# A hybrid S5 and Conformer layer: the convolution's tap diagonals get a room of their own and are made one channel block ahead

## The chip, the cores and the metric

The kernel runs on one core of one Trainium2 chip. The metric is the device time of one execution in microseconds (us), lower is better. Before the change it is 888.91 us, the median of three runs that lay between 885.72 and 889.24 us.

Engines are named as the profile names them: PE is TensorE (matmuls, with PEld for its weight loads), DVE is VectorE, ACT is ScalarE, POOL is GpSimd, and SP issues most of the transfers.

## The reference

One layer of a diffusion backbone, on 512 latent tokens and 256 context tokens of width 1024, all in float32:

```python
h = modulate(rmsnorm(x, g_mix), sh1, sc1)          # sh, sc, gt: six vectors from cond @ w_ada
z = h @ w_in                                       # 3584 columns
y_a = s5_post(s5_mixer(z[:, :512], ...))           # state-space branch, two directions, 32 groups
y_b = conv_branch(z[:, 512:1536], 8 rows, ...)     # the convolution branch
x = x + gt1 * (g_a * y_a + g_b * y_b) @ w_o        # g_a, g_b: sigmoid of the other columns of z
h = modulate(rmsnorm(x, g_ffn), sh2, sc2)
x = x + gt2 * hier_moe(h)                          # 4 groups of 8 experts, top 2 within one group
out = rmsnorm(x, g_final)
```

The part that the change is in:

```python
def conv_branch(zb, n_rows, w_dw, b_dw, ln_g, ln_b, w_out):
    v = glu(zb)                                    # 512 tokens x 512 channels
    v = v.reshape(8, 64, 512)                      # 8 grid rows of 64 tokens
    v = depthwise_conv(v, w_dw, width 31, 'SAME') + b_dw
    v = silu(layernorm(v, ln_g, ln_b))
    return v.reshape(512, 512) @ w_out
```

The convolution is depthwise: each of the 512 channels has 31 weights (taps) of its own and mixes no other channel.

## The kernel before

**Stages.** First the condition vectors, the norms and the first part of the input projection (to about 104 us); then a mixed stage (to about 400 us) in which eight blocks of the state-space branch, 24 tiles of the rest of the input projection and the convolution are interleaved; then the output projections, the routing and 32 experts.

**The convolution on PE.** The 512 channels are four channel blocks of 128 channels on the partitions. The gated input of a block stands in `vp`, 8 rows of 64 tokens with 15 zeros at both ends of each row; `vp[0]` (pool tag `ch`) holds blocks 0 and 1, `vp[1]` (tag `cl`) blocks 2 and 3. `conv_diag(j)` (L786) builds the taps of block j as small diagonal matrices on DVE: two instructions (L792), one for taps 0 to 15 (128x512) and one for taps 16 to 30 (128x480), each an identity pattern `sel32` times the weights `cwt`. `conv_taps(j)` (L795) then issues 31 x 4 = 124 matmuls at L804 (as the profile counts them 248, since a float32 matmul is two), each with one 32x32 diagonal as weights and a shifted view of `vp` as the moving operand. The four matmuls of one tap are for the four quarters of 32 channels, r = 0 to 3, and each quarter has a PSUM bank of its own: `cp0` and `cp1` from the pool tag `mm` (4 banks), `cp2` and `cp3` from the tag `tp` (2 banks). ACT copies the four banks out (L808), and `conv_sum(j)` (L811) adds up the four partial sums in each bank with PE (`pcv`, L814).

**Where it stands.** `z_tile(t)` (L754) computes one 128-column tile of the projection in 24 matmuls (`zp`, L396 to L398; as tiles z0, z1, ... below). Behind tiles 2, 4, 6 and 8 follows `conv_taps` of blocks 0, 1, 2 and 3, behind tiles 3, 5, 7 and 9 their `conv_sum` (`conv_part`, L818). PE and ACT take their instructions in the order in which the code is written, through the letters of the string at L928 (`A`, `B`, `C` are z tiles, `R` and `I` the state-space block's read and input, `P` its tables, `V`, `b`, `k` its kernels, `a` a step of the condition vector's matmul or sum). DVE, POOL and SP are ordered by a scheduler.

**What shares DVE and the banks with it.** Per state-space block, DVE takes four products of PSUM tiles with cosines and sines (L669 to L672), two scans (L681), four more products (L686 to L689) and `st` (L95). It also splits the projection's weights (`zuwl`, L752), gates `vp` (L771), and finishes the block's convolution kernel `ks`: L553 is the last reader of the bank `pk` of the tag `tp`, and its result is what SP writes out with `kd` (L554) and reads back as `m` (L558).

**Pools.** The diagonals `cdg` came from the pool tag `s2`, a ring of eight 2 KB buffers per partition that also serves `sg`, `cpt`, the state-space products and others. So a buffer of the ring can make a later instruction wait for its last reader.

Of the kernel before, what the change touches and what calls it, by code (L numbers as in the profile page):

```python
# [9 lines left out]
F32 = mybir.dt.float32  # L10
# [4 lines left out]
ALU = mybir.AluOpType  # L15
# [11 lines left out]
def hybrid_kernel(  # L27
# [9 lines left out]
    V, S, G, T, SY = nc.vector, nc.scalar, nc.gpsimd, nc.tensor, nc.sync  # L37
# [10 lines left out]
    ROWS, RW = 8, 64  # L48
    PADW = RW + 2 * HALF
# [9 lines left out]
    modp = ctx.enter_context(tc.tile_pool(name="modp", bufs=1))  # L59
# [7 lines left out]
    def t2k(name, dt=F32, cols=512, p=128):  # L67
        return sm.tile([p, cols], dt, tag="s2", name=name)
# [4 lines left out]
    def ps_mm(name, p=128):  # L73
        return ps.tile([p, 512], F32, tag="mm", name=name, bufs=4)
# [4 lines left out]
    def ps_tp(name, p=128):  # L79
        return ps.tile([p, 512], F32, tag="tp", name=name, bufs=2)  # L80
# [114 lines left out]
    sel32 = sm.tile([128, 32], F32, tag="sel32", name="sel32", bufs=1)  # L195
# [4 lines left out]
    cwt = const.tile([128, 4, 32], F32, name="cwt")  # L200
# [452 lines left out]
    def s5_ut(b):  # L653
        if b < NB:
            uts[b] = s5m.tile([128, GB, NCH], F32, tag="ut", name="ut", bufs=2)
            SY.dma_start(out=uts[b], in_=ud[b // 2, 64 * (b % 2):64 * (b % 2) + 64].rearrange("(g q) t n -> (q t) g n", q=CH))
# [67 lines left out]
        V.tensor_tensor(yl[:, j, :], y, yh.bitcast(F32)[:, j, :], op=ALU.subtract)  # L724


    vp = [modp.tile([128, 2, ROWS, PADW], F32, tag=t, name=f"vp{t}") for t in ("ch", "cl")]
    for a in vp:
        G.memset(a, 0.0)


    zt = []
# [49 lines left out]

    cdg, cpart = {}, {}

    def conv_diag(j):
        cdg[j] = []
        for k0 in (0, 16):
            n = min(16, TAPS - k0)  # L790
            t = t2k("cdg").rearrange("p (k c) -> p k c", c=32)
            V.tensor_tensor(t[:, 0:n], sel32.unsqueeze(1).to_broadcast([128, n, 32]), cwt[:, j, k0:k0 + n].unsqueeze(2).to_broadcast([128, n, 32]), op=ALU.mult)  # L792
            cdg[j].append(t)

    def conv_taps(j):  # L795
        src = vp[j // 2][:, j % 2]
        conv_diag(j)
        d = cdg.pop(j)
        banks = [ps_mm("cp0"), ps_mm("cp1"), ps_tp("cp2"), ps_tp("cp3")]
        for k in range(TAPS):  # L800
            c = 32 * (k % 4)
            for r in range(4):
                rs_ = slice(32 * r, 32 * r + 32)
                T.matmul(banks[r][c:c + 32], lhsT=d[k // 16][rs_, k % 16, :], rhs=src[rs_, :, k:k + RW], start=(k < 4), stop=(k >= TAPS - 4), skip_group_check=True)  # L804
        cpart[j] = []
        for r in range(4):
            t = t2k("cpt")
            S.activation(t, banks[r], AF.Copy)  # L808
            cpart[j].append(t)
# [7 lines left out]
    def conv_part(t):  # L817

        if 2 <= t < 10:
            (conv_sum if t % 2 else conv_taps)((t - 2) // 2)  # L820
# [62 lines left out]
    def ada(n):  # L883

        for _ in range(n):
# [3 lines left out]
                ada_step(at[0])  # L889
            at[0] += 1  # L890

    s5_ut(0)
    s5_ut(1)
    for t in range(4):
# [396 lines left out]
    n = 0  # L1291
# [133 lines left out]
    with tc.If(n_gen > 0):  # L1425
        with tc.For_i(0, n_gen, 1):
# [16 lines left out]
            n = 0  # L1443
# [15 lines left out]
            def w_part(q):  # L1459
                t = mo.tile([128, 2048], F32, tag="er", name="gw", bufs=3)[:, 0:1024]  # L1460
                if q < 4:
                    v = t.rearrange("p (k a n) -> p k a n", k=2, a=2)
                    for a in range(2):
                        SY.dma_start(out=v[:, :, a, :], in_=ws[a][256 * q:256 * q + 256].rearrange("(k p) n -> p k n", p=128))
                else:
                    SY.dma_start(out=t, in_=ws[2][128 * (q - 4):128 * (q - 4) + 128])
                return t
# [11 lines left out]
            for q in range(4):  # L1479
                t = w_part(q)  # L1480
# [11 lines left out]
            for k in range(2):  # L1492
                t = w_part(4 + k)
# [220 lines left out]
```

## Time and profile before

| | |
|---|---|
| median of three runs | 888.91 us |
| profiled execution's own time | 891.78 us |
| its span (first to last instruction) | 890.1 us |
| PE busy | 746.9 us (84%) |
| DVE busy | 465.8 us (52%) |
| POOL busy | 331.7 us (37%) |
| ACT busy | 321.7 us (36%) |
| mean granted TensorE clock | 0.943 |

The profile is of one execution, and the share of a busy engine is a mean over stages that have different limits. What matters for this change is the stage from 105 to 250 us, where the four convolution blocks stand on PE at 142, 168, 202 and 231 us. A number in brackets at a row's end is the idle time of the engine just before it, with what ended it.

### The profile page before, as it was taken

What the parts mean: (1) busy time and instruction counts of PE and PEld (TensorE: products, weight loads), DVE (VectorE), ACT (ScalarE), POOL (GpSimd) and SP (SyncE); (2) the same over time, 40 slices, a digit from 0 to 9 for tenths busy, and PEclk for the clock granted to TensorE, in tenths of its full rate; (3) what the DMA queues carried; (4) which work ended last, traced back from release to release, by engine and by line L of the source; (5) the groups of instructions that cost most, each with busy time, mean ns of one, the idle gap of its engine ahead of it and who ended that gap; (6) DMA issues with size and microseconds to landing.
All of it is one profiled execution on the core that took longest, in us unless ns stands there. A gap on an engine that the chain in (4) does not pass through costs nothing. (4 is left out here: it accounts for less than half of the span.)

```text
span 890.1 us, 14314 instructions
## 1 busy us (share of the span) xinstructions
PE 746.9 (84%) x5486; PEld 519.6 (58%) x5486; DVE 465.8 (52%) x723; ACT 321.7 (36%) x559; POOL 331.7 (37%) x293
## 2 busy tenths in 40 slices
PE   3598976988889997779999993788998988888895
PEld 0476853665566775646778872455655655555542
DVE  4948464564387797826875576133223123233254
ACT  3443611353555766637732330222112112212133
POOL 4657435343576788631610122122123122122400
PEclk9998996998988999999999996799999999999997
DMA  8926860341145546478687447999989998997042
GB/s 310 263 61 177 206 214 20 107 125 30 57 135 172 169 129 182 130 248 303 210 299 274 151 132 313 397 380 364 377 321 388 407 350 342 387 389 261 27 178 94
DMA packets 84678, 202.01 MB, mean 227 GB/s; under 512 B 12859, under 2 KB 42621, under 8 KB 74866
## 3 DMA queue, kind: packets, MB, share of 16 engines
q1 hardware_dynamic: 76754, 180.00, 57.3%
q0 software_dynamic: 5856, 12.45, 4.0%
q10 hardware_dynamic: 1984, 8.44, 3.5%
q8 instruction: 53, 0.87, 0.4%
q14 instruction: 31, 0.25, 0.1%
HBM read 180.16 MB, written 26.69 MB: 232 GB/s over the span
## 5 line engine op out<-in xcount | busy, mean ns | idle before, releaser
L1346 PE MATMUL peg<-eraw,st 128*64 128x256 f32 x1152 | 133.7, 386 | 9.5 <-PEq L1407 7.4
L1346 PEld LDWEIGHTS peg<-eraw,st 128*64 128x64 f32 x1152 | 94.7, 139 | 60.4 <-issue 34.8
L1331 DVE COPY st<-pxt 128x512 f32<-128x512 f32 x32 | 22.1, 692 | 160.0 <-PE pxt L1329 160.0
L1360 ACT ACTIVATE at<-pat 128x256 f32<-128x256 f32 x32 | 12.3, 384 | 215.8 <-PE pat L1358 215.8
L1318 POOL DMA_INDIRECT xg<-h2d,tb x32 | 30.4, 950 | 141.3 <-PE pxt L1329 129.6
L396 PE MATMUL zp<-hh,zuwh 128*128 128x512 f32 x192 | 78.7, 410 | 0.0
L398 PE MATMUL zp<-hh,zuwl 128*128 128x512 f32 x192 | 77.1, 401 | 0.5 <-POOL zuwl L752 0.3
L397 PE MATMUL zp<-hl,zuwh 128*128 128x512 f32 x192 | 76.8, 400 | 0.0
L1366 PE MATMUL ped<-eraw,at 128*64 128x512 f32 x288 | 68.9, 603 | 0.0
L98 POOL TENSOR_TENSOR adacc<-adacc,wa 128x512 f32<-128x512 f32 x30 | 47.1, 1570 | 39.9 <-ACT wa L854 37.6
L1376 DVE TENSOR_TENSOR ye<-ped,gt2h 128x512 f32<-128x512 f32 x60 | 39.0, 687 | 40.2 <-PE ped L1366 37.3
L1401 POOL DMA_INDIRECT ybuf<-ye,ixh x34 | 34.0, 999 | 69.5 <-DVE ye L1376 49.8
L1329 PE MATMUL pxt<-ident,xg 128*128 128x128 f32 x256 | 42.4, 303 | 8.1 <-DMA xg<-h2d,tb 7.4
L396 PEld LDWEIGHTS zp<-hh,zuwh 128*128 128x128 f32 x192 | 37.4, 195 | 11.9 <-issue 4.4
L398 PEld LDWEIGHTS zp<-hh,zuwl 128*128 128x128 f32 x192 | 37.2, 194 | 9.8 <-POOL zuwl L752 1.8
L397 PEld LDWEIGHTS zp<-hl,zuwh 128*128 128x128 f32 x192 | 37.1, 193 | 7.4
L1329 PEld LDWEIGHTS pxt<-ident,xg 128*128 128x128 f32 x256 | 33.6, 194 | 13.1 <-issue 8.6
L1358 PE MATMUL pat<-ident,sge 64*128 64x64 f32 x128 | 21.3, 286 | 18.9 <-PEq L1407 18.2
L1358 PEld LDWEIGHTS pat<-ident,sge 64*128 64x128 f32 x128 | 17.7, 209 | 32.7 <-PEq L1407 30.4
L1366 PEld LDWEIGHTS ped<-eraw,at 128*64 128x64 f32 x288 | 17.8, 136 | 27.2 <-issue 23.6
L98 POOL TENSOR_TENSOR vb<-vta,vtb 128x512 f32<-128x512 f32 x16 | 22.3, 1393 | 30.0 <-PE pv L533 19.1
L752 DVE TENSOR_TENSOR zuwl<-zr,zuwh 128x1024 fp32r<-128x1024 f32 x16 | 28.4, 1775 | 5.7 <-ACT zuwh L751 5.6
(494 smaller groups left out, 1666.9 us busy)
## 6 DMA issues: line engine op xcount, KB each, us to landing
eraw<-in_w_exp_gate_dram SPq DMA_DIRECT2D x24, 1024.0 KB
eraw<-in_w_exp_up_dram SPq DMA_DIRECT2D x24, 1024.0 KB
eraw<-in_w_exp_down_dram SPq DMA_DIRECT2D x24, 1024.0 KB
wa<-in_w_ada_dram SPq DMA_DIRECT2D x32, 512.0 KB
zr<-in_w_in_dram SPq DMA_DIRECT2D x12, 1024.0 KB
wa<-in_w_ada_dram SPq DMA_DIRECT2D x8, 1024.0 KB
eraw<-in_w_exp_gate_dram SPq DMA_DIRECT2D x14, 512.0 KB
eraw<-in_w_exp_down_dram SPq DMA_DIRECT2D x14, 512.0 KB
```

Source lines behind the costliest of these rows:

```text
L98: G.tensor_tensor(o, a, b, op=op)
L396: T.matmul(acc, lhsT=wh, rhs=ah, start=start, stop=False)
L397: T.matmul(acc, lhsT=wh, rhs=al, start=False, stop=False)
L398: T.matmul(acc, lhsT=wl, rhs=ah, start=False, stop=stop)
L752: (G if t in ZPOOL else V).tensor_tensor(zu[t][1], raw, zu[t][0].bitcast(F32), op=ALU.subtract)
L1318: G.indirect_dma_start(out=xg, out_offset=None, in_=h2d, in_offset=bass.IndirectOffsetOnAxis(ap=idx, axis=0), bounds_check=L - 1, oob_is_e ...
L1329: T.transpose(pt[:, k, :], xg[:, 4 * h + k:D:8], ident)
L1346: T.matmul(pg[H[c], 256 * a:256 * a + 256], lhsT=st[:, k, H[a]], rhs=r[c][k // 4][:, 256 * (k % 4):256 * (k % 4) + 256], start=(k == 0), s ...
L1358: T.transpose(pa[:, 128 * k + 64 * a:128 * k + 64 * a + 64], sg[64:128, 256 * a + k:256 * a + 256:2], ident[64:128, 64:128])
L1366: T.matmul(pd[a][H[c]], lhsT=at[:, 128 * k + 64 * a:128 * k + 64 * a + 64], rhs=r[2][k][:, 512 * c:512 * c + 512], start=(k == 0), stop=(k ...
L1376: V.tensor_tensor(y[:, 512 * a:512 * a + 512], pd[a], gt2h, op=ALU.mult)
L1401: return G.indirect_dma_start(out=ybuf.rearrange("r (c n) -> (r c) n", c=2), out_offset=bass.IndirectOffsetOnAxis(ap=ixh[:, a, e:e + 1], a ...
```

## The change

The tiles under `vp` become 2048 floats wide. Their first 1504 floats are `vp` as before, and 512 of the rest are the room of the diagonals: taps 0 to 15 in the tile `ch`, taps 16 to 30 in `cl`. There is one such room, not a ring: the diagonals of block j+1 overwrite those of block j. `conv_diag(0)` is called ahead of the mixed stage's first tiles, and `conv_diag(j + 1)` at the end of the matmuls of `conv_taps(j)`.

```diff
-    vp = [modp.tile([128, 2, ROWS, PADW], F32, tag=t, name=f"vp{t}") for t in ("ch", "cl")]
-    for a in vp:
-        G.memset(a, 0.0)
+    NVP = 2 * ROWS * PADW
+    vp, cdg = [], []
+    for t in ("ch", "cl"):
+        t = modp.tile([128, 2048], F32, tag=t, name=f"vp{t}")
+        vp.append(t[:, 0:NVP].rearrange("p (i r t) -> p i r t", i=2, r=ROWS))
+
+        cdg.append(t[:, NVP:NVP + 512].rearrange("p (k c) -> p k c", c=32))
+        G.memset(vp[-1], 0.0)
...
     def conv_diag(j):
-        cdg[j] = []
         for k0 in (0, 16):
             n = min(16, TAPS - k0)
-            t = t2k("cdg").rearrange("p (k c) -> p k c", c=32)
-            V.tensor_tensor(t[:, 0:n], sel32..., cwt[:, j, k0:k0 + n]..., op=ALU.mult)
-            cdg[j].append(t)
+            V.tensor_tensor(cdg[k0 // 16][:, 0:n], sel32..., cwt[:, j, k0:k0 + n]..., op=ALU.mult)

     def conv_taps(j):
         src = vp[j // 2][:, j % 2]
-        conv_diag(j)
-        d = cdg.pop(j)
+        d = cdg
...
+        if j < 3:
+            conv_diag(j + 1)
         cpart[j] = []
...
+    conv_diag(0)
     s5_ut(0)
```

How the scheduler orders DVE with it. The first place is DVE behind the copies `ub` (L645) that end the first projection. Before:

```order
L645 COPY ub_955<-puc_328 128x8x32
L644 COPY ub_960<-puc_328 128x8x32
L645 COPY ub_960<-puc_328 128x8x32
L524 TENSOR_SCALAR cos<-cos 128x512 [waits Activation_49]
L752 TENSOR_TENSOR zuwl<-zr_980,zuwh 128x1024 [waits DMAHW0_49,Activation_49]
L752 TENSOR_TENSOR zuwl<-zr_980,zuwh 128x1024 [waits PE_49,Activation_49]
L669 TENSOR_TENSOR a_1085<-pv_1067,cos 128x512 [waits PE_49]
```

With the change the same place reads as follows (L795 is the building of diagonals, named by the tiles `vpch` and `vpcl` that now hold them; lines behind L729 have moved by up to 5):

```order
L645 COPY ub_960<-puc_328 128x8x32
L795 TENSOR_TENSOR vpch<-sel_157,cwt 128x512
L795 TENSOR_TENSOR vpcl<-sel_157,cwt 128x480
L524 TENSOR_SCALAR cos<-cos 128x512 [waits Activation_49]
L757 TENSOR_TENSOR zuwl<-zr_982,zuwh 128x1024 [waits DMAHW0_49,Activation_49]
L757 TENSOR_TENSOR zuwl<-zr_982,zuwh 128x1024 [waits PE_49,Activation_49]
L669 TENSOR_TENSOR a_1087<-pv_1069,cos 128x512 [waits PE_49]
```

The diagonals of block 0 now stand here and wait for nothing of their own. The second place is DVE behind the state-space block 1, where the diagonals of block 0 stood before:

```order
L95 TENSOR_TENSOR st_1165<-b_1167,b_1168 64x4x64
L95 TENSOR_TENSOR vta<-bb,lv 128x512
L553 TENSOR_TENSOR ks<-pk,ks 128x16 [waits PE_49]
L792 TENSOR_TENSOR cdg<-sel_157,cwt 128x512 [waits DVE_49]
L792 TENSOR_TENSOR cdg<-sel_157,cwt 128x480 [waits DVE_49]
L847 COPY adacc<-pma 128x256 [waits PE_49]
```

and with the change:

```order
L95 TENSOR_TENSOR vta<-bb,lv 128x512
L553 TENSOR_TENSOR ks<-pk,ks 128x16 [waits PE_49]
L795 TENSOR_TENSOR vpch<-sel_157,cwt 128x512 [waits PE_49]
L795 TENSOR_TENSOR vpcl<-sel_157,cwt 128x480 [waits PE_49]
L850 COPY adacc<-pma 128x256 [waits PE_49]
```

The pair in this place is now that of block 1, and it waits for PE: for the matmuls of block 0 that read the room last. The pairs of blocks 2 and 3 stand in the same way where those of blocks 1 and 2 stood, and where the pair of block 3 stood there is none. All other rows of DVE, and the order on PE, ACT, POOL and SP, are as before. The third place is PE behind tile z2, the head of the convolution of block 0. Before:

```order
L397 MATMUL zp<-hl,zuwh 128x512
L398 MATMUL zp<-hh,zuwl 128x512
L804 MATMUL cp_1252<-vpch,cdg 32x512 [waits DVE_49,Pool_49]
L804 MATMUL cp_1253<-vpch,cdg 32x512
L804 MATMUL cp_1254<-vpch,cdg 32x512 [waits PE_49,Activation_49]
L804 MATMUL cp_1255<-vpch,cdg 32x512
L804 MATMUL cp_1252<-vpch,cdg 32x512
```

and with the change:

```order
L398 MATMUL zp<-hh,zuwl 128x512
L805 MATMUL cp_1250<-vpch 32x512 [waits Pool_49]
L805 MATMUL cp_1251<-vpch 32x512
L805 MATMUL cp_1252<-vpch 32x512 [waits PE_49,Activation_49]
L805 MATMUL cp_1253<-vpch 32x512 [waits DVE_49]
L805 MATMUL cp_1250<-vpch 32x512
```

The first matmul (bank `cp0`) no longer waits for DVE, and the fourth (bank `cp3`) now does: its wait is for L553, the last reader of the bank that `cp3` takes over from `pk`.

## Rows read from the trace of the kernel before

**Rows 1.** Waits of PE, 110 to 260 us: total, times, longest (us)

```profile
PE cp L804 <- DVE cdg L792: 16.9, 3, 12.6
PE pv L666 <- DMA ut<-ud: 2.1, 1, 2.1
```

**Rows 2.** Timeline of PE: start, length, instruction, count, idle time before

```profile
142.10 10.90 PE L804 MATMUL cp<-vpch,cdg 32*32 32x512 f32 x248 [12.58 <-DVE cdg L792]
...
168.03 8.71 PE L804 MATMUL cp<-vpch,cdg 32*32 32x512 f32 x248
...
201.73 10.19 PE L804 MATMUL cp<-vpcl,cdg 32*32 32x512 f32 x248 [3.38 <-DVE cdg L792]
...
231.20 8.71 PE L804 MATMUL cp<-vpcl,cdg 32*32 32x512 f32 x248 [0.92 <-DVE cdg L792]
241.51 1.29 PE L546 MATMUL pk<-cl,bd 64*32 64x144 f32 x32 [1.61 <-ACT cpt L808]
```

**Rows 3.** Timeline of DVE, 105 to 156 us

```profile
105.62 0.54 DVE L524 TENSOR_SCALAR cos<-cos 128x512 f32<-128x512 f32 x1
...
109.62 1.23 DVE L752 TENSOR_TENSOR zuwl<-zr,zuwh 128x1024 fp32r<-128x1024 f32 x1 [2.34 <-ACT zuwh L751]
118.22 0.69 DVE L669 TENSOR_TENSOR a<-pv,cos 128x512 f32<-128x512 f32 x1 [7.37 <-PE pv L666]
...
140.73 0.16 DVE L553 TENSOR_TENSOR ks<-pk,ks 128x16 f32<-128x16 f32 x1
140.82 2.97 DVE L792 TENSOR_TENSOR cdg<-sel,cwt 128x512 f32<-128x512 f32 x2
155.35 0.42 DVE L847 COPY adacc<-pma 128x256 f32<-128x256 f32 x1 [11.56 <-PE pma L845]
```

**Rows 4.** Timeline of SP, the transfer behind L553

```profile
140.97 0.34 SPq L554 DMA_DIRECT2D kd<-ks  x1
```

**Rows 5.** Windows: length, busy of PE, PEld, DVE, ACT, POOL; clock; DMA

```profile
142.00:153.00 11.00, 10.90 (x250) 6.62 (x252) 1.79 (x1) 0.00 (x0) 7.00 (x5) 0.78 0.12 33
168.00:177.00 9.00, 8.73 (x249) 5.32 (x248) 3.96 (x2) 0.23 (x1) 3.00 (x2) 1.00 0.38 121
202.00:212.00 10.00, 9.92 (x248) 5.44 (x219) 1.88 (x4) 0.09 (x1) 0.00 (x0) 0.85 0.01 3
...
215.00:219.00 4.00, 4.00 (x12) 3.15 (x11) 2.63 (x3) 2.97 (x8) 3.68 (x3) 0.57 0.30 79
...
242.50:246.00 3.50, 3.50 (x46) 3.26 (x34) 1.10 (x3) 1.71 (x5) 1.90 (x2) 0.51 0.12 40
```

**Rows 6.** Timeline of DVE, 165 to 234 us

```profile
169.59 2.37 DVE L95 TENSOR_TENSOR vta<-bb,lv 128x512 f32<-128x512 f32 x1
...
183.41 0.43 DVE L524 TENSOR_SCALAR cos<-cos 128x512 f32<-128x512 f32 x1 [11.45 <-ACT cos L522]
...
186.27 0.69 DVE L771 SCALAR_TENSOR_TENSOR vpcl<-sg,zp 128x512 f32<-128x512 f32 x1 [0.20 <-ACT sg L768]
...
192.75 0.42 DVE L849 TENSOR_TENSOR adacc<-adacc,pma 128x256 f32<-128x256 f32 x1
...
200.47 1.78 DVE L792 TENSOR_TENSOR cdg<-sel,cwt 128x512 f32<-128x512 f32 x2
...
207.76 0.69 DVE L95 TENSOR_TENSOR clta<-cc,lq 128x512 f32<-128x512 f32 x1 [5.18 <-PE cp L804]
...
229.37 4.51 DVE L792 TENSOR_TENSOR cdg<-sel,cwt 128x512 f32<-128x512 f32 x2
```

**Rows 7.** Timeline of ACT: the state-space block's sines, behind block 2

```profile
226.77 0.63 ACT L520 ACTIVATE cos<-sin 128x512 f32<-128x512 f32 x1
```

**Rows 8.** Windows, columns as in rows 5: the mixed stage behind the convolution

```profile
300.00:340.00 40.00, 35.31 (x304) 27.88 (x302) 31.90 (x34) 25.38 (x44) 34.85 (x24) 1.00 0.55 170
```

**Rows 9.** Waits of PE, 110 us to the end: those for loaded weights

```profile
PE pma L845 <- DMA wa<-in_w_ada_dram: 4.8, 2, 4.1
...
PE peg L1346 <- DMA eraw<-in_w_exp_down_dram: 0.4, 1, 0.4
```

More of the change, by code (lines that the diff above doesn't have):

```diff
@@ L781, in hybrid_kernel @@
         cacc[j] = t4k("cacc").rearrange("p (a n) -> p a n", a=2)
-    cdg, cpart = {}, {}
+    cpart = {}
     def conv_diag(j):
-        cdg[j] = []
         for k0 in (0, 16):
             n = min(16, TAPS - k0)
-            t = t2k("cdg").rearrange("p (k c) -> p k c", c=32)
-            V.tensor_tensor(t[:, 0:n], sel32.unsqueeze(1).to_broadcast([128, n, 32]), cwt[:, j, k0:k0 + n].unsqueeze(2).to_broadcast([128, n, 32]), op=ALU.mult)
-            cdg[j].append(t)
+            V.tensor_tensor(cdg[k0 // 16][:, 0:n], sel32.unsqueeze(1).to_broadcast([128, n, 32]), cwt[:, j, k0:k0 + n].unsqueeze(2).to_broadcast([128, n, 32]), op=ALU.mult)
     def conv_taps(j):
         src = vp[j // 2][:, j % 2]
-        conv_diag(j)
-        d = cdg.pop(j)
+        d = cdg
         banks = [ps_mm("cp0"), ps_mm("cp1"), ps_tp("cp2"), ps_tp("cp3")]
```

## The prediction

> **What bounds the kernel now.** I read the waits of PE first: in the mixed stage by far the longest of them is for the diagonals, 16.9 us in 3 times, one of 12.6; the next is 2.1 [rows 1]. PE's timeline then shows where. PE ends z2 at 129.52 and starts block 0 of the convolution at 142.10, 12.58 us later; block 1 follows z4 without a gap; block 2 waits 3.38 us, block 3 0.92 us [rows 2]. So PE sets the pace here, and DVE holds it up three times. Why DVE is late is in its own timeline: it works without a pause from 118 us, and the pair of diagonals stands at 140.82, right behind L553 at 140.73 [rows 3]. The reader is to see this neighbour: it decides what the first wait leaves behind. Last, the windows by stage: a convolution block takes 8.7 us where the granted clock is 1.00, 10.9 and 10.2 us where PE stood idle ahead of it (0.78 and 0.85) [rows 2, 5].
>
> **The pair of block 0, moved to 105.6 us.** The pair costs DVE 1.8 to 4.5 us (1.78, 2.97, 4.51 in three places, the long one while POOL works) [rows 3, 6]. In its new place it pushes back `cos`, and the two weight splits that end at 110.85. DVE then has nothing to do for 7.37 us until PE hands it the first state-space product at 118.22 [rows 3]; even 4.5 us fit into that. Cost 0; without this cover it would be at most 4.5.
>
> **Block 0: what the wait of 12.58 us becomes.** With the diagonals made, the first three matmuls can go at 129.5. The fourth cannot. Its bank is the one of `pk`, and the order of the changed kernel shows it waiting for DVE: for L553, which stays where it was in DVE's queue, behind the products, scans and `vta` of state-space block 1. All of that is released by PE at 118 us and none of it is removed. L553 runs at 140.73 for 0.16 us, and SP, which waits for the same result, issues its transfer at 140.97 [rows 3, 4]. I take 141.0 as the start of the other 121 taps: a gain of 142.1 - 141.0 = 1.1 us. Bounds: 0, if L553 is as late as the diagonals were, and 12.58, if nothing holds the taps. The idle time ahead is still over 11 us, so I leave the block its 10.90 us.
>
> The Trainium skill, "TensorE: Matmul & The Clock Gate", Part 2, step 1, states that matmuls stay in program order and that only weight loads are pulled ahead. By it the taps of the other banks can't pass the waiting fourth one and the gain is 1.1; were it otherwise, three quarters of the block could run in the gap. No row of this trace has a matmul that waits in front of ready ones, so none decides it.
>
> **Block 1.** It had no wait, so it gains 0 and starts 1.1 us earlier. The next pair (block 2) now waits for the taps that read the room, until about 175.6, and holds back `vta`, which stood at 169.59. Behind that comes `cos`, for which DVE waited 11.45 us until 183.41 [rows 6]. So 175.6 plus 4.5 for the pair and 2.4 for `vta`, 182.5, is still ahead of it. Cost 0.
>
> **Block 2.** Its pair was the last thing in a queue of DVE work (200.47). Now it is made over 20 us before. What stands in for the wait are its banks: those of `tp` go free with `adacc` steps, the last of them at 192.75 [rows 6], 5 us before z6 ends at 201.73 - 3.38 = 198.35. So the block follows z6 at once, as block 1 follows z4: gain 3.38 us [rows 2]. And with no idle time ahead it should run like block 1, 8.71 instead of 10.19 us, at clock 1.00 instead of 0.85: gain 1.48 us [rows 2, 5]. Bounds for this: 0 to 1.48.
>
> **Block 3.** Gain 0.92 us [rows 2]. Its pair waits for block 2's last taps, about 206 us with all shifts, and with 2 to 4.5 us is done by 211. Behind it is `clta`, which stood at 207.76 because its ring buffer was held by these very taps [rows 6]; it gets free of that. The chain behind it ends in ACT's sines, which stood at 226.77 [rows 7]: a cover of some 10 us with all shifts.
>
> **Nothing is added.** Eight builds stay eight builds, and PE, ACT, POOL and SP keep their order. The ring `s2` is taken eight times less; being eight long, it stands behind block 3 as before.
>
> **The sum.** 1.1 + 0 + 3.38 + 1.48 + 0.92 = 6.9 us. What PE gains by 231 us should reach the end: later it waits for loaded weights only 4.8 us, and in the experts 0.4 [rows 9]; the other waits are for engines whose work PE itself releases. The profiled execution took 891.78 us (span 890.1), so 884.9; against the median of the runs, 888.91, which is 2.9 lower, I take off the same amount: **882.0 us**.
>
> **What stays open in it.** Behind a block PE waits some 1.6 us for the copies of its banks [rows 2]. After two of the three gaps a slow stretch followed, 4.0 us at clock 0.57 and 3.5 at 0.51 [rows 5], each a loss of about 1.7 us (4.0 x 0.43); after block 1 none did. All work behind shifts by 1 to 7 us, so one more stretch could come (1.7 dearer) or both go (3.4 cheaper).
>
> The Trainium skill, same page, Part 1, says that the slow matmuls at a start differ in number between runs of one kernel. By that the three gaps are throws anew in each run; one more slow one makes the gain 5.2. The trace agrees so far that equal gaps had unequal ends.
>
> **The rivals.**
> 1. *The whole wait of block 0 goes* (the bank is free in time, or the taps pass it): 12.58 + 3.38 + 0.92 + 1.48 = 18.4 us, and block 0 keeps the clock, 10.90 - 8.71 = 2.2: 20.6 us, 868.3 us. For it speaks only that the profile names the diagonals as what ended the wait; against it, that L553 ended 0.2 us before that in the same queue. 4%.
> 2. *The gain is eaten behind the convolution.* From 300 to 340 us DVE and POOL are nearly as busy as PE (31.9, 34.9 and 35.3 of 40 us) [rows 8], and an engine that doesn't start earlier, or the transfers that PE waits 4.8 us for [rows 9], would swallow part of it. If 4.8 us are given back there: 2.1 us left, 886.8. Against it: DVE waited for others 11.56 us behind block 0 and 11.45 us behind block 1 [rows 3, 6], so it has no backlog when the convolution ends. The same comes out if the copies that end in slow stretches get one more and block 2 keeps its low clock. 21%.
> 3. *Slower: the waiting pairs hold up DVE's queue.* One room means that a pair waits for the last taps of the block before, and then takes up to 4.5 us with DVE's whole queue behind it. It decides if what stands behind is wanted by PE before the pair is through: at block 1 if the pair ends later than 183.4, since `vpcl` at 186.27 is what block 2 works on [rows 6]. If the three pairs stood open on PE's path, 3 x 4.5 = 13.5 us against the gain of 6.9: 895.5 us. Against it: 7 us of slack at block 1, and behind block 0 DVE's next work is an `adacc` step for which it waited 11.56 us until 155.35 [rows 3]. 7%.
>
> **How the numbers follow.** My forecast has 68%; by the slow stretches alone it lies between 878.6 and 883.7, and the three runs before lay 3.5 us apart, so I give it 878 to 886. Over all cases I take 877 to 888.5: rival 2 inside, most of rivals 1 and 3 outside, some 2 in 10 left out. Half a per cent, 4.4 us, is about what a measurement can tell from no change. So faster is below 884.5: most of the forecast (0.57 of 0.68) and rival 1, 0.61. Same: the rest of the forecast and rival 2, 0.32. Slower: rival 3, 0.07.
>
> **What the profile would show.** Right: three taps at about 129.5, then idle until about 141 ended by `ks` L553 and not by diagonals; block 2 directly behind z6, 8.7 us long; no wait for diagonals anywhere; the pairs on DVE starting when taps end. Wrong, if block 0 starts much before 140 us (rival 1); if PE's experts start less than 4 us earlier though the convolution ends 7 earlier (rival 2); if a z tile or a block waits for `zuwl`, `vpcl` or `cos` behind a pair (rival 3).

## The result and the profile after

The changed kernel takes 880.24 us, the median of 9 runs (877.05 to 883.66), against 888.91 us for the kernel before (9 runs, 884.94 to 890.52). The ratio is 0.9889, with a 95% interval of 0.9865 to 0.9913: faster by 1.1%. The profiled execution of the changed kernel took 880.24 us with a span of 878.5 and a granted clock of 0.959; before it was 891.78, 890.1 and 0.943. So the two spans lie 11.6 us apart and the medians 8.7; the forecast was 6.9 us.

First the waits of PE from 110 to 260 us, which answer to [rows 1] (columns as there):

```profile
PE cp L805 <- DVE ks L553: 9.8, 1, 9.8
PE pv L533 <- DVE adb L871: 5.3, 1, 5.3
...
```

No wait for diagonals is left. In its place stands the wait for L553, the last reader of the bank that the fourth tap matmul takes over. (The second row is not new: before, that wait, 4.21 us long, lies just behind this window, at 265 us.) PE's timeline shows all four blocks, as [rows 2] did:

```profile
128.64 1.73 PE L805 MATMUL cp<-vpch 32*32 32x512 f32 x6
140.14 5.96 PE L805 MATMUL cp<-vpch 32*32 32x512 f32 x110 [9.77 <-DVE ks L553]
...
145.96 4.78 PE L805 MATMUL cp<-vpch,vpcl 32*32 32x512 f32 x116
...
165.56 4.08 PE L805 MATMUL cp<-vpch 32*32 32x512 f32 x115
...
196.59 4.08 PE L805 MATMUL cp<-vpcl,vpch 32*32 32x512 f32 x115
...
200.52 4.77 PE L805 MATMUL cp<-vpcl 32*32 32x512 f32 x117
...
222.66 4.08 PE L805 MATMUL cp<-vpcl,vpch 32*32 32x512 f32 x115
...
232.99 1.21 PE L546 MATMUL pk<-cl,bd 64*32 64x144 f32 x32 [1.61 <-ACT cpt L811]
```

Six matmuls (the first three as the code counts them), then 9.77 us of idle time, then the rest of block 0. Blocks 2 and 3 follow the z tile ahead of them without a gap. (A block is now cut into several rows, because the profile groups by the tiles that hold the diagonals.) DVE's timeline, to be held against [rows 3, 6]:

```profile
106.47 0.68 DVE L795 TENSOR_TENSOR vpch<-sel,cwt 128x512 f32<-128x512 f32 x1
...
117.85 0.69 DVE L669 TENSOR_TENSOR a<-pv,cos 128x512 f32<-128x512 f32 x1 [6.20 <-PE pv L666]
...
139.93 0.16 DVE L553 TENSOR_TENSOR ks<-pk,ks 128x16 f32<-128x16 f32 x1
...
146.59 1.77 DVE L795 TENSOR_TENSOR vpch<-sel,cwt 128x512 f32<-128x512 f32 x1 [6.50 <-PE cp L805]
...
150.80 0.66 DVE L795 TENSOR_TENSOR vpcl<-sel,cwt 128x480 f32<-128x480 f32 x1 [2.44 <-PE cp L805]
...
174.38 0.66 DVE L795 TENSOR_TENSOR vpcl<-sel,cwt 128x480 f32<-128x480 f32 x1 [3.57 <-PE cp L805]
...
180.95 0.43 DVE L524 TENSOR_SCALAR cos<-cos 128x512 f32<-128x512 f32 x1 [4.93 <-ACT cos L522]
...
206.32 0.69 DVE L95 TENSOR_TENSOR clta<-cc,lq 128x512 f32<-128x512 f32 x1
```

The two tiles of a pair each wait for those taps of the block before that read them, and DVE then still waits for others, for `cos` 4.93 us. `clta` no longer waits for taps. The windows of the four blocks, in the order of the blocks, answer to [rows 5]:

```profile
140.00:151.00 11.00, 10.86 (x248) 6.39 (x250) 2.06 (x4) 0.46 (x1) 7.49 (x6) 0.80 0.13 38
165.50:174.30 8.80, 8.77 (x249) 5.33 (x248) 0.69 (x1) 0.00 (x0) 2.14 (x2) 1.00 0.37 122
196.50:205.50 9.00, 8.79 (x249) 5.33 (x248) 3.11 (x4) 0.17 (x1) 2.87 (x3) 1.00 0.01 4
222.60:231.50 8.90, 8.78 (x249) 5.32 (x248) 0.24 (x1) 1.41 (x3) 3.66 (x2) 1.00 0.09 33
233.00:236.50 3.50, 3.44 (x76) 2.92 (x78) 1.34 (x4) 2.14 (x6) 1.05 (x1) 1.00 0.09 31
```

Block 2 has clock 1.00 where it had 0.85. The stretch behind block 3 (last row) has 1.00 where it had 0.51; but a second profile of the kernel before (experiment 7) has 1.00 there too, so this difference is not the change's.

**Where the 11.6 us are.** Positions in PE's timelines, in us. The second pair are the same two kernels, profiled once more. An expert's end is the start of its transposition `pat`.

| | before | after | difference | second pair, difference |
|---|---|---|---|---|
| end of block 3 | 239.9 | 231.4 | -8.5 | -7.6 |
| last `po` matmul (output projection) | 536.4 | 530.2 | -6.2 | -5.0 |
| from there to the first expert's `pat` | 37.9 | 36.0 | -1.9 | -2.0 |
| from there to the last expert's `pat` | 276.8 | 276.9 | +0.1 | +0.5 |
| from there to the end | 39.0 | 35.5 | -3.5 | -3.4 |

The last 5.4 us come from a place that the prediction does not speak of: the experts and the tail behind them, whose code is unchanged. The experiments were for two questions: which part of the change brings the gain up to `po`, and what the experts have to do with it.

### The profile page after: what moved, and what is told of

Same layout as the page of the kernel before. It is cut to its first block, busy times and chain, and to the rows that moved or that the text cites. A ratio compares the mean times of both kernels' runs of the same rounds, so it can differ in the third digit from the quotient of the medians.

```text
span 878.5 us, 14308 instructions
## 1 busy us (share of the span) xinstructions
PE 738.2 (84%) x5486; PEld 513.4 (58%) x5486; DVE 458.5 (52%) x723; ACT 321.2 (37%) x559; POOL 329.6 (38%) x293
```

## The experiments

**1. Pair 0 alone in the room.** Blocks 1 to 3 take their diagonals from the ring, as before.

```diff
+        if j > 0:
+            d = [t2k("cdg")... for _ in range(2)]
+            conv_diag(j, d)
...
+    conv_diag(0, cdg)
```

> Only the diagonals of block 0 are made ahead, in the room; blocks 1 to 3 build theirs in the ring at their own place, as before the change. Theory 1 (block 0 passes from the diagonals to L553, the neighbour in DVE's queue): block 0 starts 1 to 2 us earlier, blocks 2 and 3 wait 3.4 and 0.9 us for their pairs as before; 1 to 2 us faster than before, about 887 us. Rival (the gain of the change comes from block 0's long wait of 12.6 us): most of the 8.7 us of the change, about 881 us.

Measured: 885.42 us, ratio 0.9927 (0.9901 to 0.9954). PE's timeline:

```profile
141.06 5.45 PE L808 MATMUL cp<-vpch 32*32 32x512 f32 x111 [9.77 <-DVE ks L553]
...
199.58 11.38 PE L808 MATMUL cp<-vpcl,cdg 32*32 32x512 f32 x248 [3.37 <-DVE cdg L795]
```

Block 0 starts 1.0 us earlier, block 2 waits 3.37 us as before: the stages are as expected, and the last `po` matmul stands only 1.5 us earlier than in the first profile of before (534.9). But the time fell by 6.5 us. From that matmul to the end it takes 346.7 us, where before took 353.7. This was the first sign that the part behind `po` had got faster without the convolution.

**2. The call for pair 0 back in its old place**, the rest as in the change; meant to leave block 0's wait as it was.

```diff
     def conv_taps(j):
+        if j == 0:
+            conv_diag(0)
...
-    conv_diag(0)
     s5_ut(0)
```

> Only the diagonals of blocks 1 to 3 are made one block ahead, in the room; the pair of block 0 is built in its own place behind L553. Theory 1: block 0 starts at 142 us as before, the waits of blocks 2 and 3 go and block 2 keeps its clock; 5.8 us faster than before (3.38 + 0.92 + 1.48), 883 us, and with the slow stretches that did not come in the profile of the change up to 3 us more. Rival (gain from block 0): no more than 2 us faster, 887 us.

Measured: 880.75 us, ratio 0.9870 (0.9838 to 0.9902). The premise failed, as DVE's timeline shows:

```profile
107.35 0.68 DVE L795 TENSOR_TENSOR vpch<-sel,cwt 128x512 f32<-128x512 f32 x1
```

The scheduler makes pair 0 at 107 us all the same. What had held it was the ring: its two buffers had readers in the state-space block. So this run only repeats the change.

**3. The room alone.** All four calls at the head of their own blocks again.

```diff
+        conv_diag(j)
         d = cdg
...
-        if j < 3:
-            conv_diag(j + 1)
```

> Only the room: each pair is called for at the head of its own block again, as before, not one block ahead. Theory 1 (the scheduler places DVE's work by what it waits for; what held a pair back was the ring's buffer, whose last readers are other DVE work, and the call's place in the program decides nothing): the pairs stand in DVE's queue where they stand in the changed kernel, but for pair 0 one or two instructions later; ratio 0.987 to 0.990, no wait of PE for diagonals. Rival (the one-ahead call is what takes the pairs off PE's path): PE waits for pairs at blocks 1 to 3 after the taps of the block before, 1.8 to 4.5 us each where no other work lies between, and the ratio is 0.995 or more.

Measured: 879.50 us, ratio 0.9889 (0.9857 to 0.9921). PE waits for no pair, and the pairs stand in DVE's queue as expected. Of the change's two halves, the room is all; the call one block ahead does nothing that the runs can show.

**4. Pair 0 in the ring, pairs 1 to 3 in the room**: what experiment 2 had failed to set apart.

```diff
+        if j == 0:
+            d = [t2k("cdg")... for _ in range(2)]
+            conv_diag(0, d)
```

> Block 0's pair of diagonals stays in the ring and where it stood before in DVE's queue, right behind L553; pairs 1 to 3 are in the room, made ahead. That is the half of the change that the experiment before failed to set apart. Theory 1 (by stages): block 0 waits 12.6 us for the diagonals again and starts at about 142; block 2 has no wait (3.4) and runs 8.7 us (10.2 before), block 3 no wait (0.9). The gain up to block 3 is 3.4 + 1.5 + 0.9 = 5.8 us of the change's 8.5 there, and the time about 883 us, ratio 0.993. Rival (the gain hangs mostly on block 0's start): block 3 starts less than 3 us earlier than before, ratio 0.998.

Measured: 879.22 us, ratio 0.9875 (0.9843 to 0.9906), 4 us better than expected. The timeline of PE:

```profile
141.92 10.50 PE L808 MATMUL cp<-vpch,cdg 32*32 32x512 f32 x248 [12.58 <-DVE cdg L795]
```

Block 0 waits its full 12.58 us again, and the kernel is no slower than the change. Block 3 ends at 232.5 us (239.9 and 239.2 in the profiles of before). So the rival falls: the gain up to `po` hangs mostly on blocks 2 and 3. That block 0's 1.1 us are worth nothing does not follow: this kernel is spared a wait of PE for ACT behind z5, 0.47 us as in before against 1.24 in the change, which nearly makes up for them (see the part on blocks 2 and 3 below).

**5. The bank of the fourth tap set free.** The changed kernel; ACT copies the last columns of `pk` too, so that L553 reads no PSUM any more.

```diff
+        S.activation(ks[:, 7], pk[0][:, 128:144], AF.Copy)
...
-        V.tensor_tensor(ks[:, 7], pk[0][:, 128:144], ks[:, 15], op=ALU.add)
+        V.tensor_tensor(ks[:, 7], ks[:, 7], ks[:, 15], op=ALU.add)
```

> The change, and ACT copies the 16 columns that L553 reads from the bank of pk, so that L553 reads SBUF alone and the bank is free some 10 us earlier (one more ACT copy of 0.2 us in each of the 8 blocks). Theory 1 (that bank is what holds block 0): block 0 starts at about 130 us directly behind z2 instead of 140, runs at the high clock (8.8 instead of 10.4 us), and the kernel is about 10 us faster than the change, 870 us. Rival (DVE's own work up to 140 us is wanted by PE right behind block 0, so the wait only moves): block 0 starts early, but the step behind it waits, and less than 3 us is gained over the change.

Measured: 872.57 us, ratio 0.9778 (0.9752 to 0.9805). It beats both kernels. PE's timeline:

```profile
129.89 4.79 PE L806 MATMUL cp<-vpch 32*32 32x512 f32 x117
...
134.53 4.76 PE L806 MATMUL cp<-vpch,vpcl 32*32 32x512 f32 x115
```

Block 0 runs right behind z2. The diagonals were ready; the bank alone held back the other 121 taps.

**6. The same edit in the kernel before.**

> The kernel before, with the same copy by ACT and nothing else. Theory 1 (two things stand at the same end of DVE's queue, the bank and the diagonals, and each alone holds block 0): the diagonals still come at 142 us, no change, 887 to 890 us. Rival (the bank alone held block 0): as much faster as c_bank is against the change, about 879 us.

Measured: 896.67 us, ratio 1.0048 (1.0028 to 1.0068), slower. PE's timeline:

```profile
143.95 10.84 PE L805 MATMUL cp<-vpch,cdg 32*32 32x512 f32 x248 [12.65 <-DVE cdg L793]
```

Without the room the wait is still for the diagonals, and the free bank is worth nothing: the two waits are in parallel, and only both edits together remove the time. That the kernel is slower was not expected: in its profile block 0 starts 1.9 us and the last `po` matmul 4.2 us later than in the first profile of before. Which of the eight added copies costs this, and how, stays open.

**7. Both kernels once more**, unchanged, profiled on one chip. (The expectations from here on count the tail from an earlier point: their 49.1 and 45.6 us are the 39.0 and 35.5 of the table above.)

> The kernel before, word for word, profiled once more beside a profile of the changed kernel on the same chip. The question is the part of the gain that the waits of the convolution don't explain: PE's busy time was 8.7 us less in the changed kernel with the same 5486 instructions, and the stretch from the last ybuf transposition to the end took 45.6 us instead of 49.1. Theory 1 (where a slow stretch falls is fixed by the kernel's own timing): this profile shows the same slow stretches as the first of before, at 142, 215 and 242 us and in the tail, PE busy 746 to 750 us, the tail 49 us. Rival (the slow stretches are thrown anew in each execution): the tail takes 45.6 us or PE's busy time lies below 743 us, and the stretches behind the blocks fall elsewhere. The time itself: ratio 1.000, by both.

> The changed kernel, word for word, profiled once more. Theory 1 (slow stretches fixed by the kernel's timing): PE busy 738 to 740 us, the tail 45.6 us, block 2 of the convolution 8.7 to 8.9 us, no slow stretch behind block 3 (234 us); ratio 0.989. Rival (thrown anew): a tail of 47 to 49 us or a slow stretch behind a block, and PE busy above 743 us; the ratio is still 0.989 in the mean, the gain of 6.9 us of the waits and 2 to 3 us that go with the chance of fewer stretches.

Measured: 1.0017 (0.9997 to 1.0037) and 0.9893 (0.9869 to 0.9917). The second profiles give the last column of the table above: what lies behind `po` repeats to 0.1 us at the first expert and in the tail, so it belongs to the kernels, as theory 1 has it. The stretches inside the mixed stage move, as the rival has it: block 2 of before ran 11.4 us instead of 10.2, and behind blocks 2 and 3 no slow stretch came. PE's busy time was 745.8 and 741.1 us, just outside what theory 1 gave for each.

**The place.** The first expert in the kernel before, PE and then ACT:

```profile
558.54 1.94 PE L1329 MATMUL pxt<-ident,xg 128*128 128x128 f32 x8 [7.38 <-DMA xg<-h2d,tb]
561.65 6.18 PE L1346 MATMUL peg<-eraw,st 128*64 128x256 f32 x32 [1.17 <-ACT st L1333]
```

```profile
559.71 1.28 ACT L1333 ACT_TABLE_LOAD   x1 [19.11 <-PE pxt L1329]
...
561.00 0.60 ACT L1333 ACTIVATE st<-pxt 128x512 f32<-128x512 f32 x1
```

and in the changed kernel:

```profile
552.40 1.94 PE L1333 MATMUL pxt<-ident,xg 128*128 128x128 f32 x8 [7.65 <-DMA xg<-h2d,tb]
554.27 5.26 PE L1350 MATMUL peg<-eraw,st 128*64 128x256 f32 x32
```

```profile
545.25 1.28 ACT L1337 ACT_TABLE_LOAD   x1 [11.08 <-DVE tb L1283]
553.52 0.60 ACT L1337 ACTIVATE st<-pxt 128x512 f32<-128x512 f32 x1 [6.99 <-PE pxt L1333]
```

Before, ACT's table load of 1.28 us starts when the transposed tokens `pxt` are there, and PE waits 1.17 us for what follows it. With the change it starts while the tokens are still on their way, and PE waits for nothing. The orders of the built programs show why (a row, its line, what it waits for); before:

```
400 L1333 ACT_TABLE_LOAD [waits DVE_49,PE_49]
401 L1333 ACTIVATE st<-pxt 128x512 [waits Activation_49]
```

and with the change:

```
400 L1337 ACT_TABLE_LOAD
401 L1337 ACTIVATE st<-pxt 128x512 [waits PE_49]
```

The copy waits for three engines before, and two of the three waits stand in front of the table load. With the change it waits for PE alone, behind the load. The waits come from memory: the first `st` tile lies partly where a buffer of the ring `s2` lay. In the memory map of the program before, that buffer was last held by `mi` of the last routing step; with the change by `rsc` of the second of the four steps, which ACT is past. So the ring did not come out the same: its eight buffers don't go round in turn (they were handed out 32 to 36 times each before, 30 to 37 times after), and eight requests fewer change who gets which.

**8. The table load alone, in the kernel before.** A one-element copy ahead of the first expert takes it.

```diff
+        S.activation(itr[:, 1:2], itr[:, 2:3], AF.Copy)
         st[0] = new_st()
```

> The kernel before, and one thing alone: a one-element copy on ACT ahead of the first expert takes the ACT_TABLE_LOAD of 1.28 us off the path (before, it stands between the last transposition of the first expert's tokens and the copy st<-pxt, at 559.71, and PE waits 1.17 us for it; in all seven kernels with the room it stands 8 us earlier, and PE doesn't wait). The diagonals and the convolution are untouched. Theory 1 (the part of the gain behind po comes from this load: 353.6 us from the last po matmul to the end in before and in its second profile, 346.5 to 349.0 in the seven): PE goes from pxt to peg without the wait, the clock comes back some 3 us earlier, the tail takes 45.6 us instead of 49.1, the stretch from po to the end about 348.7, and the time is about 885.5 us, ratio 0.994 to 0.996. Rival (the slow tail has another reason): only the wait of 1.2 us goes, the tail stays 49 us, ratio 0.998 to 1.000.

> The kernel before with the table load alone moved off the path, a second time. In its first profile the first expert came 2.2 us sooner (35.8 us behind the last po matmul instead of 38.0), as the changed kernel's does (36.0); one longer expert at 137 us (10.2 instead of 8.5 us) took it back, and the tail was slow as in before. Theory 1 (the load is worth 2 us at the first expert; where slow stretches fall behind it is chance of one execution): the first expert at 35.8 to 36.0 again, the longer expert elsewhere or nowhere; ratio 0.994 to 0.998. Rival (the slow stretches belong to the kernel): the longer expert at 137 us and the slow tail again, ratio 0.997 to 1.000.

Measured: 0.9938 (0.9911 to 0.9965) and, the second time, 0.9955 (0.9929 to 0.9981). ACT and PE in the first profile:

```profile
551.69 1.28 ACT L1621 ACT_TABLE_LOAD   x1 [12.07 <-DVEq L1425]
559.08 0.60 ACT L1333 ACTIVATE st<-pxt 128x512 f32<-128x512 f32 x1 [5.89 <-PE pxt L1329]
```

```profile
557.89 1.94 PE L1329 MATMUL pxt<-ident,xg 128*128 128x128 f32 x8 [7.70 <-DMA xg<-h2d,tb]
559.76 4.66 PE L1346 MATMUL peg<-eraw,st 128*64 128x256 f32 x32
```

The wait is gone, and the first `pat` stands 35.8 and 35.9 us behind `po`, where before has 37.9 and 38.0. By the times the kernel is faster by this one instruction. But the tail is 37.3 and 38.9 us, not 35.5: that part of the expectation is a miss. And in both profiles the 2 us are given back at one place. The expert at 137 us behind `po` takes 10.2 and 10.0 us from its `pat` to the next, 8.5 in before; its `ped`, in the first profile and in before:

```profile
674.28 3.57 PE L1366 MATMUL ped<-eraw,at 128*64 128x512 f32 x8
```

```profile
677.25 1.94 PE L1366 MATMUL ped<-eraw,at 128*64 128x512 f32 x8
```

From 147 us on the experts stand where before has them, to 0.2 us, up to the last but one, and from `po` to the end it takes 353.4 and 353.5 us, against 353.7 and 353.6 in before. So in the second run the rival was right about the long expert and the slow tail, and theory 1 about the time. The two profiled executions were the slowest of the 8 and of the 12. Where the others gain their 0.4 to 0.6 per cent, the profiles do not show.

**9. The table load put back, in the changed kernel.** Two more buffers of the ring are taken behind the last routing step, so that `st` again waits for three engines.

```diff
             route(3)
+            pad = [t2k("pad") for _ in range(2)]
+            V.memset(pad[0][:, 0:1], 0.0)
+            S.activation(pad[1][:, 0:1], pad[0][:, 0:1], AF.Copy)
+            V.memset(pad[1][:, 1:2], 0.0)
```

> The changed kernel, and one thing alone: two more buffers of the ring are taken behind the last routing step (two one-column clearings on DVE, one one-element copy on ACT), so that the memory of the first expert's st tile was last held by work of DVE and ACT, as in the kernel before; the table load then stands behind the wait for pxt again. The room and the diagonals are as in the changed kernel. Theory 1: PE waits about 1.2 us for ACT's st at the first expert, the clock comes back later, the tail takes about 49 us, po to the end 353 us, the time about 885.5 us, ratio 0.994 to 0.996 to before, so half of the change's gain is given back. Rival: ratio 0.990 to 0.991, the tail 45.6 us.

> The changed kernel with the table load put back behind the wait, a second time. Theory 1: the first expert at 38.4 us behind the last po matmul again (36.0 in the changed kernel), ratio 0.991 to 0.993, 2 us or 0.0025 above the changed kernel's 0.989; the tail as chance has it. Rival (the load decides the tail too): a tail of 49 us and 0.994 to 0.996.

Measured: 0.9901 (0.9868 to 0.9933) and 0.9911 (0.9884 to 0.9938). ACT and PE in the first profile:

```profile
554.54 1.28 ACT L1341 ACT_TABLE_LOAD   x1 [14.77 <-PE pxt L1337]
```

```profile
553.38 1.94 PE L1337 MATMUL pxt<-ident,xg 128*128 128x128 f32 x8 [7.75 <-DMA xg<-h2d,tb]
556.49 6.39 PE L1354 MATMUL peg<-eraw,st 128*64 128x256 f32 x32 [1.17 <-ACT st L1341]
```

The wait of 1.17 us is back, and the first `pat` stands at 38.4 us in both profiles. Against the change's 0.9889 and 0.9893 that gives back 0.0008 to 0.0022 in time (some 1 to 2 us), and the intervals overlap with the change's own, so the time alone would not show it. The tail is 37.3 and 37.2 us, between the two kernels.

So the load is worth about 2 us at the first expert, shown in both directions. In the changed kernel they last: the 13th expert's `pat` stands at 145.5 us behind `po`, in before at 147.4. In experiment 8's profiles they don't. The load does not settle the tail either, of which more below. Nor is it all that moves the first expert: in experiments 1, 3 and 4 its `pat` stands at 34.1 to 34.4 us, because there the last `plog` (eight matmuls of the routing) and what hangs on it ran sooner: 1.08 to 1.09 us (clock 1.00 in experiment 3) instead of 1.93 in the other profiles (0.50 in the change). What decides that was not found.

## Why the prediction was right, step by step

Single profiles differ by a few us from one execution to the next, so the terms are best held against means: over the four profiles with the convolution of before (two of before, two of experiment 8) and the six with that of the change (two of the change, experiments 2 and 3, two of experiment 9).

| term | forecast | measured |
|---|---|---|
| block 0, rest of the taps starts | -1.1 | 141.90 to 140.75: -1.15 |
| block 2 starts (with the term above) | -4.5 | 201.24 to 197.39: -3.85 |
| block 2, length | -1.48 (bounds 0 to -1.48) | 10.76 to 8.71: -2.05 |
| block 3 starts (all terms) | -6.9 | 230.96 to 223.96: -7.00 |
| last `po` matmul | -6.9 | 536.54 to 530.76: -5.78 |

- **Block 0: right.** The bank of `pk` takes over the wait, and L553 at 139.93 ends it. Experiments 5 and 6 show that it is the bank, by taking it away with the room and without. Rival 1 is refuted.
- **The order on PE.** Six matmuls went, then PE stood for 9.77 us, though three quarters of the taps behind the waiting one are for banks that were free. That agrees with the rule weighed in the prediction (the Trainium skill, "TensorE: Matmul & The Clock Gate", Part 2, step 1: matmuls stay in program order).
- **Blocks 2 and 3: right, but a smaller wait came in ahead of block 2.** Both waits for diagonals went. But behind z5 PE now waits 1.24 us for ACT's `cacc`, where it waited 0.48; that is why block 2 starts only 3.85 us earlier. Before, z5's last matmul and PE's wait, and ACT's table load ahead of z5's sigmoid `sg`:

```profile
184.71 0.39 PE L398 MATMUL zp<-hh,zuwl 128*128 128x512 f32 x1
...
186.92 0.72 PE L546 MATMUL pk<-cl,bd 64*32 64x144 f32 x30 [0.48 <-ACT cacc L815]
```

```profile
184.35 1.28 ACT L768 ACT_TABLE_LOAD   x1
```

and with the change:

```profile
182.25 0.39 PE L398 MATMUL zp<-hh,zuwl 128*128 128x512 f32 x1
...
185.23 0.72 PE L546 MATMUL pk<-cl,bd 64*32 64x144 f32 x30 [1.24 <-ACT cacc L818]
```

```profile
182.71 1.28 ACT L773 ACT_TABLE_LOAD   x1 [0.83 <-issue]
```

Before, the load starts ahead of z5's end; with the change, behind it. It is the effect of the first expert's load, the other way round: the ring `s2` gives `sg` another buffer. In the built program of before `sg` waits for DVE ahead of the load and for PE (z5) behind it; with the change DVE and PE stand ahead of the load, and POOL, which used that buffer too, behind it. All six profiles with the change's convolution have 1.24 us; the four with that of before, and experiment 4, have 0.47 or 0.48.

- **Block 2's clock: right, but more than was allowed for.** It ran 10.1 to 11.4 us in the four profiles, 8.7 in all six, a gain of 2.05 where the prediction's upper bound was 1.48. That block 3 comes out at 7.00 against 6.9 is luck in part: 0.6 too much here stands against 0.65 too little at block 2's start.
- **The pairs that hold DVE's queue: right.** A pair costs 1.3 to 2.4 us, and DVE waits for `cos` behind it. Rival 3 is refuted: no z tile and no block waits for what stands behind a pair.
- **Given back behind the convolution (rival 2): in part.** Of 7.0 us at block 3, 5.8 arrive at `po`; but the last `po` matmul lies anywhere between 535.2 and 538.5 us in the four profiles and 528.6 and 533.6 in the six, so 1.2 us is hardly clear of chance. In the first pair 2.3 us are given back, in two waits: the one for `adb` (5.33 us instead of 4.21) and the one that the prediction named, for the weights `wa` (5.9 instead of 4.8 [rows 9]):

```profile
PE pma L848 <- DMA wa<-in_w_ada_dram: 5.9, 2, 3.3
```

In the mean the wait for `wa` went from 5.2 to 5.6 us. (The rival's last sentence is mis-added: one more slow stretch and no gain in block 2's clock leave 6.9 - 1.7 - 1.48 = 3.7 us, not 2.1.)

- **What failed: "Nothing is added. [...] The ring `s2` is taken eight times less; being eight long, it stands behind block 3 as before."** It does not. Who holds which buffer is another matter from how many were taken. At z5 that puts a table load on PE's path (0.76 us lost), and 370 us later it takes one off it (2.0 us won). Both are terms that the sum lacks.
- **The tail: not foreseen, and open.** The same eight matmuls (`fin`, `ped`, `yr`) near the end, in before and then with the change:

```profile
876.14 2.58 PE L1588 MATMUL fin<-yr,ident 128*128 128x512 f32 x4 [2.42 <-DVE yr L1586]
879.37 3.78 PE L1588 MATMUL ped<-yr,ident 128*128 128x512 f32 x4 [0.65 <-DVE yr L1586]
```

```profile
866.39 1.98 PE L1592 MATMUL fin<-yr,ident 128*128 128x512 f32 x4 [2.42 <-DVE yr L1590]
869.62 1.99 PE L1592 MATMUL ped<-yr,ident 128*128 128x512 f32 x4 [1.25 <-DVE yr L1590]
```

and the windows of these stretches:

```profile
876.00:883.20 7.20, 6.36 (x8) 1.85 (x8) 4.65 (x10) 3.60 (x10) 0.00 (x0) 0.60 0.43 174
```

```profile
866.30:871.70 5.40, 3.97 (x8) 1.35 (x8) 4.51 (x10) 3.64 (x10) 0.00 (x0) 1.00 0.42 171
```

Before, `ped` takes nearly twice as long: the granted clock is 0.60 over the stretch, mostly the level of 1.2 GHz, behind the same wait of 2.42 us after which the changed kernel goes on at 2.4 GHz (1.00). The tail took 38.9 to 39.0 us in both profiles of before and in experiment 6, and 35.5 to 35.8 in all seven with a room and an early table load (the change twice, experiments 1 to 5). With the load moved in either direction it took 37.2 to 38.9. So neither the load nor the room decides it by itself. What does was not found; a run of before with idle time added ahead of the experts would say whether the time that has passed does.

By the medians the gain is 8.7 us, by the ratio 9.9 (0.0111 x 888.91): 5.8 up to `po`, 2.0 at the first expert, and a rest of 0.9 to 2.1. The tail's 3.4 in the profiles would more than fill it; how much of it is in the runs without a profile is not shown. So the time came out near the 882.0 for reasons that are only in part the prediction's.

## What to carry to other kernels

A buffer that is ready early is worth only as much as the next thing that the same instruction waits for: look for the second wait in the queue that released the first, and remove both (experiment 5, 0.9778, against 0.9889 and 1.0048 for each alone). With a scheduler, giving a tile memory of its own moves the work; moving the call need not. When a change takes requests out of a shared ring, compare the waits of all instructions behind it, and look at what stands first in each later stage: the difference can come out far from the edit, in either direction, and can be had alone (experiment 8, 0.9938 and 0.9955, though its profiles do not show where).

## What was not expected of the hardware

At the first expert an ACT_TABLE_LOAD of 1.28 us costs PE nothing or 2.0 us, depending on whether the waits of the instruction that needs it stand behind it or ahead of it: 1.17 us of it as PE's wait, and some 0.9 us because the matmuls behind the wait ran longer at the low clock (6.18 us at clock 0.59 and 6.39 at 0.57, against 4.66 at 0.78 and 5.26 at 0.69, for the same 32 `peg` matmuls). And one stretch of matmuls in the tail, behind the same wait of 2.42 us, ran mostly at the low level of the clock in one kernel (0.60) and at the high one in the other (1.00).
